# First phase of a hybrid layer: accumulators spilled through ScalarE and GpSimd, and the shift of the modulation summed on VectorE from the fourth block on

## The chip, the cores and the metric

The kernel runs on one core of a Trainium2 chip. The metric is the device time of one execution in microseconds. PE is TensorE, DVE VectorE, ACT ScalarE, POOL GpSimd, SP the queue that issues most of the loads.

## What is computed

One layer of a diffusion backbone on 256 latent tokens and 256 context tokens of 4096 channels, all float32. Cut to what matters here:

```python
mod_l = silu(c) @ w_ada + b_ada            # shift, scale and gate, 3 x 4096, for the latent tokens
mod_c = silu(c_ctx) @ w_ada + b_ada        # the same for the context tokens
hl = rmsnorm(xl, norm_g) * (1.0 + sc_l) + sh_l
hc = rmsnorm(xc, norm_g) * (1.0 + sc_c) + sh_c
# hl @ w_in and hc @ w_in: nine groups of columns; then convolution, recurrence and attention on them,
# the output projection, the gate g_l and a last rmsnorm
```

Shift and scale of a channel are needed before that channel's row of `w_in` can be used in a product, and they cost two columns of `w_ada` each, 134 MB in all.

## The kernel before, in words

**Phases.** The first phase (to about 941 us of the profile) computes r_x and v of both kinds of tokens and k of the context. The second phase computes the other columns of `w_in` with the convolution, the recurrence and the attention beside them, the third the output projection. Only the first phase is touched by the change, but for one buffer size.

**Blocks.** In the first phase the contraction over 4096 channels, 32 tiles of 128, is cut into ten blocks (`BLOCKS`: 1, 2, 3, 3, 3 and five of 4 tiles, counted from 0 here). In each block ten chunks of 512 columns are multiplied: two of kind "r" and four of "k" by `gemm_cm` (line 342), four of "v" by `gemm_tm` (line 361). A chunk leaves its result in four PSUM banks (r, v) or two (k), 32 in each block. `bank` gives the products five PSUM banks in turn. `spill` (line 492) moves a chunk's banks into accumulators `acc` in SBUF: in block 0 by a ScalarE copy (line 497), in all others by a VectorE addition that reads the bank and the accumulator (line 499).

**Weights.** `weights` loads `w_in` through SP into buffers `raw` (`NRAW` of them, shared with the loads of `w_ada`), and splits each pair of tiles into a high part on ScalarE (`hi`, line 338) and a low part on VectorE (`lo`, line 339). Each product runs as three passes over these parts. There are three buffers of `hi` and three of `lo`.

**Modulation.** `ada_units` (line 165) makes units of one load of up to 1 MB of `w_ada` each. A unit's work is either products on TensorE (line 217, tile `psa`, the two vectors as stationary columns) or, with `on_vector`, eight VectorE instructions that add a scaled row to one of two accumulators `gacc` (lines 160 and 162, one of each pair for the latent and one for the context vector). The finish `fin_` sends the sums through transposes on TensorE (line 175, tile `psm`; one set for `psa`, two sets for `gacc`) and reduces them on VectorE (lines 177 and 179). Part 0 of a block is the scale (`modG`), part 1 the shift (`modS`). Units of the next blocks are emitted between the products of this one by `background`, at a rate of 2.15 times the chunk's weight less 1.2. When both parts of a block are there, `make_h` (line 314) computes the normalised, modulated tokens of it (tiles `h`, `ch`, `lh`, lines 320 to 322).

**Order.** Every engine runs its instructions in the order that a scheduler wrote at build time; work within `hp()` is put as early as it can be. Pages of 2 KB a partition (`page`, `NPG` of them) hold the accumulators, tokens and all else that lives for a while.

**Last block.** In it `aside` puts the recurrence of the first heads among the chunks; its gate weights `gw` are loaded from GpSimd's queue (lines 425 and 426), and the sums for the gate g_l begin on VectorE (line 245).

Of the kernel before, what the change touches and what calls it, by code (L numbers as in the profile page):

```python
# [17 lines left out]
P = 128  # L18
# [6 lines left out]
    0, 1024, 2048, 3072, 4096, 5120, 7168, 9216, 11264)  # L25
# blocks of the contraction in the first phase, in tiles of 128
BLOCKS = [1, 2, 3, 3, 3, 4, 4, 4, 4, 4]
# from this block on, every second one's shift is summed on the vector engine
PAIRED = 8
# pages of 2 KB, buffers of weights as loaded and as split  # L30
NPG, NRAW, NHI = 75, 3, 3
# tiles of the contraction kept for the second half of the last chunk
HELD = 12
# urgency of what the tensor engine waits for
HP = 200000
# rates of the loads that go beside the products, by phase
ADA_A, ADA_B, CAP = 2.15, 1.2, 4.0
G1, G2, G3 = 0.4, 0.3, 0.4
# chunks of the last block that a recurrence follows; order of the second phase
REC1 = (1, 2, 4, 6, 8)  # L40
# [4 lines left out]
def tile_hybrid_layer(ctx: ExitStack, tc: tile.TileContext, x, c, cctx_tok, c_ctx, w_ada, b_ada,  # L45
                      norm_g, w_in, conv_w, conv_b, ln_g, ln_b, w_pw, b_pw, rconv_w, rconv_b,
                      w_r, b_r, w_i, b_i, lam, rpb, w_out, final_g, masks, out):
    nc = tc.nc
# [10 lines left out]
    def background(weight):  # L59
        """emits queued units of loads between those of the products, at the set rate"""  # L60
        bg["credit"] = min(bg["credit"] + bg["rate"](weight), CAP)
        while bg["q"] and bg["credit"] >= 2.0:
            bg["credit"] -= 2.0
            bg["q"].pop(0)()
# [17 lines left out]
    V, A, S, G = nc.vector, nc.scalar, nc.sync, nc.gpsimd  # L82
# [39 lines left out]

    # silu(c), silu(c_ctx) as channel columns, padded to 32 stationary columns
    scol = cp.tile([P, 64], F32, name="scol")
# [30 lines left out]
    def accumulate(k, w, n, which):  # L155
        """gacc[b] += silu(vector b)[k] * w on the vector engine"""
        for b in which:
            a, s = gacc[b][:, :n], scol[:, 32 * b + k:32 * b + k + 1]
            if k == 0:
                V.tensor_scalar(a, w, s, None, ALU.mult)  # L160
            else:
                V.scalar_tensor_tensor(a, w, s, a, ALU.mult, ALU.add)

# [1 line left out]
    def ada_units(k0, s, parts=(0, 1), on_vector=False):  # L165
# [92 lines left out]
    def rsqrt(y, v, t):  # L258
        """y = v ** -0.5, the table's root refined by a Newton step"""
        A.activation(y, v, AF.Sqrt)  # L260
        V.reciprocal(y, y)
        V.tensor_mul(t, y, y)
        V.tensor_mul(t, t, v)
        V.tensor_scalar(t, t, -0.5, 1.5, ALU.mult, ALU.add)
        V.tensor_mul(y, y, t)

# [1 line left out]
    ss = cp.tile([P, 4, 8], F32, name="ss")  # L268
# [56 lines left out]

# [1 line left out]
    def weights(view, ks, c0):  # L327
        """tiles of the weights, up to 4 loaded and 2 split at a time: [(tiles of the contraction, high, low)]"""
        for i in range(0, len(ks), 4):
            kp = ks[i:i + 4]  # L330
            raw = wp.tile([P, 4, 512], F32, name="raw", tag="raw", bufs=NRAW)
            S.dma_start(raw[:, :len(kp)], view[:, kp[0]:kp[0] + len(kp), c0:c0 + 512])
            for o in range(0, len(kp), 2):
                n = min(2, len(kp) - o)
                hi = wp.tile([P, 2, 512], F32R, name="hi", tag="hi", bufs=NHI)
                lo = wp.tile([P, 2, 512], F32R, name="lo", tag="lo", bufs=NHI)
                with hp():
                    A.copy(hi[:, :n], raw[:, o:o + n])  # L338
                    V.tensor_sub(lo[:, :n], raw[:, o:o + n], hi[:, :n].bitcast(F32))  # L339
                yield kp[o:o + n], hi, lo  # L340

    def gemm_cm(view, ks, c0, movs):
        """channel-major: out[n, t] for 4 tiles of n and each moving operand, 256 columns a region"""
        nb = 2 * len(movs)
        banks = [bank("g", "gcm") for _ in range(nb)]
        for kp, wh, wl in weights(view, ks, c0):
            for nt in range(4):
                for j, k in enumerate(kp):
                    last = k == ks[-1]
                    seq = [(wh, m, 0) for m in range(len(movs))] + [(wh, m, 1) for m in range(len(movs))] + \  # L350
                          [(wl, m, 0) for m in range(len(movs))]
                    for qi, (w, m, part) in enumerate(seq):
                        r = nt * len(movs) + m
                        first = k == ks[0] and qi < len(movs) and r % 2 == 0
                        nc.tensor.matmul(banks[r // 2][:, (r % 2) * T:(r % 2) * T + T],  # L355
                                         w[:, j, nt * P:(nt + 1) * P], movs[m][k][:, part],
                                         start=first, stop=last and qi >= 2 * len(movs), skip_group_check=True)
            background(len(movs))
        return banks

    def gemm_tm(view, ks, c0, stats, end=True):
        """token-major: out[t, n] for each stationary operand, 512 columns"""
        banks = [bank("g", "gtm") for _ in stats]
# [20 lines left out]
    def columns():  # L384
# [4 lines left out]
        V.tensor_scalar(hpw, col("b_pw", 0, 8), 0.5, None, ALU.mult)  # L389
        # 4 softplus(-lam), softplus(-lam) = (max(-lam, 0) + log1p(exp(-|lam|))), log1p(e) = 2 atanh(e / (2 + e))  # L390
        lm = col("lam", 0, 16)
# [21 lines left out]
    def ybs(n):  # L413
        """where the two directions' sum of head n lies: half a page of the inputs of a pair of heads"""
        return acc[("r", n // 4), n % 4 // 2 * 2][:, (n % 2) * T:(n % 2) * T + T]

    def recurrence(n):
# [22 lines left out]
        for d in range(2):  # L440
# [6 lines left out]
            A.activation(ti, pi, AF.Tanh, bias=hbi[:, ci:ci + 1], scale=0.5)  # L447
            # 2 sigmoid(z) = exp(min(z, 0)) (1 + |tanh(z / 2)|)
            A.activation(e, pr, AF.Relu, bias=nbr[:, ci:ci + 1], scale=-1.0)
# [31 lines left out]

# [1 line left out]
    acc = {}  # L483
    side = [lambda n=n: recurrence(n) for n in range(8)]

    def aside(n=1):
        """emits the next pieces of work that need few products, among the chunks of those that need many"""
        for _ in range(n):
            if side:
                side.pop(0)()  # L490

    def spill(banks, key):
        for i, b in enumerate(banks):
            with hp():
                if (key, i) not in acc:
                    acc[key, i] = page([P, 512], name="acc")
                    A.copy(acc[key, i], b)
                else:
                    V.tensor_add(acc[key, i], acc[key, i], b)  # L499

# [4 lines left out]
    while bi < len(BLOCKS):  # L505
        if bi < PAIRED:
            aq += ada_units(starts[bi], BLOCKS[bi])
        else:
            # the second block's shift is summed on the vector engine, spread among the other three parts
            pe = ada_units(starts[bi], BLOCKS[bi]) + [lambda bi=bi: done.add(bi)]  # L510
            bi += 1
            pe += ada_units(starts[bi], BLOCKS[bi], parts=(0,))
            ve = ada_units(starts[bi], BLOCKS[bi], parts=(1,), on_vector=True)
            for i, u in enumerate(pe):
                aq.append(u)
                n = len(ve) * (i + 1) // len(pe) - len(ve) * i // len(pe)
                aq += ve[len(ve) * i // len(pe):][:n]
        aq.append(lambda bi=bi: done.add(bi))
        bi += 1
# [37 lines left out]

# [1 line left out]
    ALLK = list(range(KT))  # L559
# [7 lines left out]
    def silu2(b):  # L567
        """2 silu(b), a page"""
        t = page([P, 512], name="sil")
# [50 lines left out]

    # queries lie from right to left within a grid row, so that the bias rows are read with a stride of +1
    def att_group(g):
# [120 lines left out]

# [1 line left out]
    korder = list(range(16, 32)) + list(range(8, 16)) + list(range(8))  # L745
# [3 lines left out]
    for oc in range(8):  # L749
# [27 lines left out]
        if oc < 7:  # L777
# [4 lines left out]
            continue  # L782
        # last chunk: the second token tile comes behind the first by HELD tiles of the contraction
        gate()
# [37 lines left out]
def _window():  # L822
    """neighbourhood mask by shape alone: rows are (query row parity, query column from the right),
    columns are key columns; a factor and an addend"""
    qc = 63 - np.arange(P) % 64
# [27 lines left out]
```

## Time and profile before

| | us |
|---|---|
| median of 3 runs | 2377.08 |
| lowest and highest | 2374.56, 2380.82 |
| span of the profiled execution, first to last instruction | 2371.5 |
| what lies around the span, median less span | 5.6 |
| TensorE busy | 2315.1 |
| VectorE busy | 1580.3 |
| ScalarE busy | 945.7 |
| GpSimd busy | 95.8 |

The page gives no other time for the profiled execution than its span; the table sets it beside the median. TensorE's ends of instructions are modelled, so that its work is read from the distance of starts and not from its busy share.

### The profile page before, as it was taken

The numbers are of one execution on the slowest core, as the hardware profiler recorded it, in microseconds if no ns is written. First come the engines' busy times: TensorE is split into PE (matmuls) and PEld (weight loads), VectorE is DVE, ScalarE is ACT, GpSimd is POOL, SyncE is SP. The second block draws the span as 40 slices with busy tenths as digits, with TensorE's granted clock in tenths as the row PEclk, the third lists the DMA queues.
The fourth block names the chain that finished last, engine by engine and source line by source line (L and its number), as shares of the span: only waits on it lengthen the run. The fifth ranks groups of instructions, "written<-read, shape, count | busy, mean of one in ns | idle before, by whom it ended". The sixth has DMA issues, their size and how long they took to land.

```text
span 2371.5 us, 38433 instructions
## 1 busy us (share of the span) xinstructions
PE 2315.1 (98%) x16013; PEld 2034.4 (86%) x16013; DVE 1580.3 (67%) x2289; ACT 945.7 (40%) x1228; POOL 95.8 (4%) x150
## 2 busy tenths in 40 slices
PE   6899999999999999999999999999999999999997
PEld 4667777777788998999999899999999999888886
DVE  4465545445778779987879596955766666665555
ACT  5322212222223246886433343344444434434444
POOL 0000000000000001000000101101001001000000
PEclk9999999999999999999999999999999999999999
DMA  9888788877877544656776767767576678775664
GB/s 312 270 279 272 254 298 298 295 266 252 295 269 258 192 163 174 222 183 213 245 233 203 188 215 202 204 215 188 182 245 171 207 265 301 264 263 187 191 192 173
DMA packets 293461, 551.27 MB, mean 232 GB/s; under 512 B 10959, under 2 KB 52647, under 8 KB 293287
## 3 DMA queue, kind: packets, MB, share of 16 engines
q1 hardware_dynamic: 287856, 536.91, 66.1%
q0 software_dynamic: 4480, 11.54, 4.3%
q8 instruction: 125, 2.05, 0.3%
q10 hardware_dynamic: 951, 0.37, 0.1%
q14 instruction: 49, 0.40, 0.0%
HBM read 544.58 MB, written 4.19 MB: 231 GB/s over the span
## 4 chain that ended last, share of the span: by engine, by line
PE 83%; DMA 8%; DVE 4%; ACT 3%; issue 1%; SPq 0%; DVEq 0%; ACTq 0%
PE gcm L355 48%; PE gtm L371 9%; PE gtm L372 8%; PE gtm L370 8%; PE psa L217 5%; DMA raw<-in_w_ada_dram 4%; DMA raw<-in_w_in_dram 3%; DVE lo L339 2%; PE y L614 1%; ACT hi L338 1%; DMA xp<-in_ctx_dram 1%; DVE gacc L245 1%; PE pt L607 1%; PE sc L593 0%; PE sc L594 0%
## 5 line engine op out<-in xcount | busy, mean ns | idle before, releaser
L339 DVE TENSOR_TENSOR lo<-raw,hi 128x1024 fp32r<-128x1024 f32 (+1 forms) x630 | 747.4, 1189 | 556.8 <-ACT hi L338 552.9
L338 ACT CAST hi<-raw 128x1024 fp32r<-128x1024 f32 (+1 forms) x630 | 640.1, 1022 | 1171.9 <-PE gcm L355 492.8
L355 PE MATMUL gcm<-lh,hi 128*128 128x256 f32 x5632 | 1069.5, 285 | 2.9 <-ACT hi L338 2.8
L355 PEld LDWEIGHTS gcm<-lh,hi 128*128 128x128 f32 x5632 | 896.8, 192 | 18.3 <-issue 13.4
L355 PE MATMUL gcm<-lh,lo 128*128 128x256 f32 x2816 | 796.2, 285 | 4.2 <-DVE lo L339 4.0
L355 PEld LDWEIGHTS gcm<-lh,lo 128*128 128x128 f32 x2816 | 537.8, 192 | 11.6 <-DVE lo L339 5.8
L355 PE MATMUL gcm<-ch,hi 128*128 128x256 f32 x1536 | 326.6, 287 | 3.4 <-ACT hi L338 2.3
L355 PEld LDWEIGHTS gcm<-ch,hi 128*128 128x128 f32 x1536 | 259.0, 191 | 36.3 <-issue 27.8
L245 DVE SCALAR_TENSOR_TENSOR gacc<-raw,scol,gacc 128x512 f32<-128x512 f32 x248 | 185.8, 749 | 49.6 <-DMA raw<-in_w_ada_dram 47.1
L355 PE MATMUL gcm<-ch,lo 128*128 128x256 f32 x768 | 217.6, 286 | 0.0
L371 PE MATMUL gtm<-lo,mix 128*128 128x512 f32 x488 | 192.0, 393 | 0.1
L372 PE MATMUL gtm<-hi,mix 128*128 128x512 f32 x488 | 190.1, 390 | 0.0
L370 PE MATMUL gtm<-hi,mix 128*128 128x512 f32 x488 | 171.1, 390 | 0.0
L355 PEld LDWEIGHTS gcm<-ch,lo 128*128 128x128 f32 x768 | 146.5, 191 | 12.8 <-issue 9.0
L217 PE MATMUL psa<-raw,cpad 128*32 128x512 f32 (+3 forms) x1216 | 132.5, 521 | 7.9 <-DMA raw<-in_w_ada_dram 7.8
L499 DVE TENSOR_TENSOR acc<-acc,gcm 128x512 f32<-128x512 f32 x144 | 96.1, 682 | 37.7 <-PE gcm L355 37.1
L371 PEld LDWEIGHTS gtm<-lo,mix 128*128 128x128 f32 x488 | 91.6, 188 | 20.5 <-DVE lo L339 1.3
L370 PEld LDWEIGHTS gtm<-hi,mix 128*128 128x128 f32 x488 | 91.5, 188 | 19.2
L499 DVE TENSOR_TENSOR acc<-acc,gtm 128x512 f32<-128x512 f32 x144 | 94.3, 680 | 19.9 <-PE gtm L372 19.7
L372 PEld LDWEIGHTS gtm<-hi,mix 128*128 128x128 f32 x488 | 91.7, 188 | 18.4
L673 DVE SCALAR_TENSOR_TENSOR cv<-upad,cols,cv 128x256 f32<-128x256 f32 x240 | 105.6, 483 | 0.0
L371 PE MATMUL gtm<-lo,ch 128*128 128x512 f32 x256 | 102.2, 399 | 0.2 <-DVE lo L339 0.2
(218 smaller groups left out, 2107.9 us busy)
## 6 DMA issues: line engine op xcount, KB each, us to landing
raw<-in_w_in_dram SPq DMA_DIRECT2D x210, 1024.0 KB, 5.2
raw<-in_w_ada_dram SPq DMA_DIRECT2D x156, 1024.0 KB, 5.5
raw<-in_w_out_dram SPq DMA_DIRECT2D x61, 1024.0 KB, 5.5
raw<-in_w_ada_dram SPq DMA_DIRECT2D x48, 768.0 KB, 5.9
raw<-in_w_in_dram SPq DMA_DIRECT2D x30, 768.0 KB, 6.1
raw<-in_w_in_dram SPq DMA_DIRECT2D x10, 512.0 KB, 5.4
xp<-in_ctx_dram SPq DMA_DIRECT2D x16, 256.0 KB, 5.8
xp<-in_x_dram SPq DMA_DIRECT2D x16, 256.0 KB, 5.4
```

What stands on the lines that cost most here:

```text
L217: nc.tensor.matmul(st["ps"][32 * q:32 * q + 32, :W], cpad[k // 16][:, k % 16, :], raw[:, j, :], start=(k < 4), stop=(k >= KT - 4))
L245: V.scalar_tensor_tensor(st["a"], raw[:, j], s, st["a"], ALU.mult, ALU.add)
L338: A.copy(hi[:, :n], raw[:, o:o + n])
L339: V.tensor_sub(lo[:, :n], raw[:, o:o + n], hi[:, :n].bitcast(F32))
L355: nc.tensor.matmul(banks[r // 2][:, (r % 2) * T:(r % 2) * T + T], w[:, j, nt * P:(nt + 1) * P], movs[m][k][:, part], start=first, stop=las ...
L370: nc.tensor.matmul(banks[b], hh, wh[:, j], start=first, stop=False)
L371: nc.tensor.matmul(banks[b], hh, wl[:, j], start=False, stop=False)
L372: nc.tensor.matmul(banks[b], hl, wh[:, j], start=False, stop=last)
L499: V.tensor_add(acc[key, i], acc[key, i], b)
L607: nc.tensor.transpose(ps[:, kt * T + qt * P:kt * T + qt * P + P], Ps[qt][:, (2 * kp + kt) * P:(2 * kp + kt + 1) * P], ident)
L614: nc.tensor.matmul(ps[:, :T], acc[("v", h // 4), kt][:, i * P:(i + 1) * P], Ps[kt // 2][:, (kt % 2) * T:(kt % 2) * T + T], start=(kt == 0) ...
L673: V.scalar_tensor_tensor(o, upad[n][:, tap:tap + T], cw(tap, n), o, ALU.mult, ALU.add)
```

## The change

Three things are done to the first phase, and two sizes make room for them.

- `spill` no longer adds on VectorE. From block 1 on each bank is copied to a page `sum` by ScalarE (line 500 of the changed kernel), and GpSimd adds that page to the accumulator (line 501).
- The shift of every block from 3 on is summed on VectorE. Before, that was so for block 9 alone, and the shifts of blocks 3 to 8 went to TensorE.
- Units of the scale (TensorE) and of the shift (VectorE) of one block now alternate.
- Buffers `raw` go from 3 to 4 and pages from 75 to 77; the memory comes from the scratch of the DMAs that GpSimd issues, set to 4096 bytes.

```diff
-PAIRED = 8
+ON_VECTOR = 3
-NPG, NRAW, NHI = 75, 3, 3
+NPG, NRAW, NHI = 77, 4, 3
...
                     A.copy(acc[key, i], b)
                 else:
-                    V.tensor_add(acc[key, i], acc[key, i], b)
+                    t = page([P, 512], name="sum")
+                    A.copy(t, b)
+                    G.tensor_add(acc[key, i], acc[key, i], t)
...
-        if bi < PAIRED:
+        if bi < ON_VECTOR:
             aq += ada_units(starts[bi], BLOCKS[bi])
         else:
-            pe = ada_units(starts[bi], BLOCKS[bi]) + [lambda bi=bi: done.add(bi)]
-            bi += 1
-            pe += ada_units(starts[bi], BLOCKS[bi], parts=(0,))
+            pe = ada_units(starts[bi], BLOCKS[bi], parts=(0,))
             ve = ada_units(starts[bi], BLOCKS[bi], parts=(1,), on_vector=True)
-            for i, u in enumerate(pe):
-                aq.append(u)
-                n = len(ve) * (i + 1) // len(pe) - len(ve) * i // len(pe)
-                aq += ve[len(ve) * i // len(pe):][:n]
+            for i in range(len(ve)):
+                aq += pe[len(pe) * i // len(ve):len(pe) * (i + 1) // len(ve)]
+                aq.append(ve[i])
         aq.append(lambda bi=bi: done.add(bi))
         bi += 1
...
-    nc = _bacc.Bacc("TRN2", target_bir_lowering=False, num_devices=1)
+    nc = _bacc.Bacc("TRN2", target_bir_lowering=False, num_devices=1, dynamic_dma_scratch_size=4096)
```

VectorE in the middle of the first phase, blocks of four tiles. Before, the low parts (`lo`) stand between additions of PSUM banks to accumulators:

```order
L499 TENSOR_TENSOR acc_588<-acc_588,gcm_3859 128x512
L339 TENSOR_TENSOR lo<-raw,hi 128x1024 x2
L499 TENSOR_TENSOR acc_620<-acc_620,gcm_3988 128x512
L499 TENSOR_TENSOR acc_622<-acc_622,gcm_3989 128x512
L339 TENSOR_TENSOR lo<-raw,hi 128x1024
L170 COPY adas_120<-psa_3845 128x512
L339 TENSOR_TENSOR lo<-raw,hi 128x1024
L499 TENSOR_TENSOR acc_656<-acc_656,gtm_4056 128x512
```

Of the change, the low parts stand between the sums of the shift:

```order
L339 TENSOR_TENSOR lo<-raw,hi 128x1024
L162 SCALAR_TENSOR_TENSOR gacc_126<-raw,scol,gacc_126 128x512
L339 TENSOR_TENSOR lo<-raw,hi 128x1024
L162 SCALAR_TENSOR_TENSOR gacc_125<-raw,scol,gacc_125 128x512
L162 SCALAR_TENSOR_TENSOR gacc_126<-raw,scol,gacc_126 128x512
L179 TENSOR_REDUCE sums_4532<-psm_4533 128x8
L339 TENSOR_TENSOR lo<-raw,hi 128x1024
L183 TENSOR_TENSOR modG<-sums_4532,cols 128x8
```

The additions of banks have left VectorE's queue, and instructions that read two operands from SBUF (`raw` and `gacc`) stand in their place.

ScalarE at the same place. Before, its queue holds the high parts and little else:

```order
L338 CAST hi<-raw 128x1024
L321 ACTIVATE ch_4657<-h_4656,modS 128x256
L338 CAST hi<-raw 128x1024 x11
L321 ACTIVATE lh_4658<-h_4656,modS 128x256
L321 ACTIVATE ch_4666<-h_4665,modS 128x256
```

Of the change, the copies of a chunk's banks (`gcm` two, `gtm` four) stand between the high parts:

```order
L338 CAST hi<-raw 128x1024
L500 COPY sum_5555<-gtm_5472 128x512
L500 COPY sum_5558<-gtm_5473 128x512
L500 COPY sum_5561<-gtm_5474 128x512
L500 COPY sum_5564<-gtm_5475 128x512
L338 CAST hi<-raw 128x1024 x2
L500 COPY sum_5637<-gcm_5567 128x512
L338 CAST hi<-raw 128x1024
L500 COPY sum_5640<-gcm_5568 128x512
```

A high part now waits behind copies, and these wait for the chunk's last product and for a free page.

GpSimd at the end of the first phase. Before, the loads of the recurrence's gate weights are its first work after the memsets at the start:

```order
L133 MEMSET cpad_100 128x512
L152 MEMSET adas_119 128x512
L152 MEMSET adas_120 128x512
L152 MEMSET junk_121 128x512
L425 DMA gw_7680<-in_w_r_dram 128x128
L426 DMA gw_7680<-in_w_i_dram 128x128
```

Of the change, these loads stand among the additions of the last block:

```order
L425 DMA gw_8422<-in_w_r_dram 128x128
L426 DMA gw_8422<-in_w_i_dram 128x128
L501 TENSOR_TENSOR acc_620<-acc_620,sum_8534 128x512
L501 TENSOR_TENSOR acc_622<-acc_622,sum_8537 128x512
L425 DMA gw_8423<-in_w_r_dram 128x128
L426 DMA gw_8423<-in_w_i_dram 128x128
```

There are 288 such additions on GpSimd, and in the last block some of them stand behind a load that waits until an earlier head's gate weights have been used.

## Rows read from the trace of the kernel before

**Rows 1.** Busy time and share of the span by engine, whole execution.

```profile
PE 2315.1 (98%) x16013; PEld 2034.4 (86%) x16013; DVE 1580.3 (67%) x2289; ACT 945.7 (40%) x1228; POOL 95.8 (4%) x150
```

**Rows 2.** Busy time in four stretches, all engines: block 1, blocks 2-7, 8, 9.

```profile
core 0: us, PE busy (x) PEld busy (x) DVE busy (x) ACT busy (x) POOL busy (x), PEclk, DMA share, GB/s
95.00:165.40 70.40, 67.33 (x461) 48.49 (x460) 43.40 (x96) 14.18 (x18) 0.00 (x0) 0.98 0.82 271
165.40:756.70 591.30, 590.57 (x3871) 450.95 (x3870) 349.54 (x535) 135.83 (x173) 1.57 (x3) 1.00 0.81 278
756.70:849.00 92.30, 92.30 (x601) 84.73 (x600) 64.86 (x84) 22.06 (x21) 0.70 (x2) 1.00 0.56 196
849.00:941.50 92.50, 92.50 (x550) 79.87 (x549) 81.20 (x116) 52.30 (x66) 7.52 (x14) 1.00 0.47 163
```

**Rows 3.** The same view of line 499 alone (VectorE), blocks 2-7.

```profile
165.40:756.70 591.30, 126.66 (x193) 1.00 0.81 278
```

**Rows 4.** TensorE in order of time (start, duration, line, tiles), around modulation products.

```profile
126.31 0.39 PE L371 MATMUL gtm<-lo,lh 128*128 128x512 f32 x1
126.63 0.85 PE L217 MATMUL psa<-raw,cpad 128*32 128x384 f32 x8
127.41 0.50 PE L372 MATMUL gtm<-hi,lh 128*128 128x512 f32 x1
127.75 0.39 PE L370 MATMUL gtm<-hi,lh 128*128 128x512 f32 x1
...
399.86 0.28 PE L355 MATMUL gcm<-lh,hi 128*128 128x256 f32 x1
399.98 0.28 PE L355 MATMUL gcm<-ch,hi 128*128 128x256 f32 x1
400.19 1.06 PE L217 MATMUL psa<-raw,cpad 128*32 128x512 f32 x8
401.19 0.38 PE L355 MATMUL gcm<-lh,hi 128*128 128x256 f32 x1
401.41 0.28 PE L355 MATMUL gcm<-ch,lo 128*128 128x256 f32 x1
```

**Rows 5.** VectorE in order of time: seven sums of the shift.

```profile
603.58 4.73 DVE L162 SCALAR_TENSOR_TENSOR gacc<-raw,scol,gacc 128x512 f32<-128x512 f32 x7 [3.87 <-DMA raw<-in_w_ada_dram]
```

**Rows 6.** VectorE's groups, blocks 2-7: busy, mean ns | idle before, releasers.

```profile
L339 DVE TENSOR_TENSOR lo<-raw,hi 128x1024 fp32r<-128x1024 f32 x92 | 112.4, 1223 | 177.3 <-ACT hi L338 177.3
L162 DVE SCALAR_TENSOR_TENSOR gacc<-raw,scol,gacc 128x512 f32<-128x512 f32 x62 | 43.1, 744 | 6.7 <-DMA raw<-in_w_ada_dram 6.6
L339 DVE TENSOR_TENSOR lo<-raw,hi 128x512 fp32r<-128x512 f32 x29 | 19.9, 687 | 5.0 <-ACT hi L338 4.9
```

**Rows 7.** One line's instructions: duration ns min/median/max, first and last start.

```profile
L497 ACT COPY acc<-gcm x16: 579/590/616, 52.1 to 80.9; 128x512 f32<-128x512 f32 x16
...
L588 POOL TENSOR_TENSOR B<-B,mask x16: 992/1010/1982, 1223.8 to 1803.6; 128x384 f32<-128x384 f32 x16
```

**Rows 8.** GpSimd's groups, whole execution: busy, mean ns | idle before.

```profile
L133 POOL MEMSET cpad<- 128x512 f32 x2 | 1.0, 519 | 0.0
...
L679 POOL MEMSET om<- 128x128 f32 x1 | 0.2, 205 | 0.0
```

**Rows 9.** GpSimd and VectorE in order of time where both run, second phase.

```profile
1524.53 2.85 POOL L587 TENSOR_TENSOR B<-B,mask 128x384 f32<-128x384 f32 x1 [6.55 <-DMA B<-in_rpb_dram]
1527.46 1.08 POOL L588 TENSOR_TENSOR B<-B,mask 128x384 f32<-128x384 f32 x1
...
1525.29 1.22 DVE L339 TENSOR_TENSOR lo<-raw,hi 128x1024 fp32r<-128x1024 f32 x1
1526.42 2.40 DVE L673 SCALAR_TENSOR_TENSOR cv<-upad,cols,cv 128x256 f32<-128x256 f32 x2
...
1466.01 0.88 DVE L673 SCALAR_TENSOR_TENSOR cv<-upad,cols,cv 128x256 f32<-128x256 f32 x2
...
1802.38 1.18 POOL L587 TENSOR_TENSOR B<-B,mask 128x384 f32<-128x384 f32 x1 [5.41 <-DMA B<-in_rpb_dram]
...
1802.59 1.52 DVE L245 SCALAR_TENSOR_TENSOR gacc<-raw,scol,gacc 128x512 f32<-128x512 f32 x1
```

## The prediction

> **What bounds the kernel now.** I read the shares first: TensorE is busy 98% of the span, VectorE 67%, ScalarE 40%, GpSimd 4% [rows 1]. Since TensorE's ends are modelled, I then looked at its starts in the first phase: 256-column products start every 0.12 us (399.86, 399.98) and 512-column ones every 0.23, without gaps [rows 4]. In blocks 2 to 7, 591.3 us, TensorE is busy 590.6 at a granted clock of 1.00, VectorE 349.5 (59%), ScalarE 135.8, GpSimd idle but for 1.6, the DMA engines at 0.81 [rows 2]. So TensorE sets the pace there; whatever leaves it is gained for as long as all others keep up, and VectorE has 242 us to spare. Block 9 is different: VectorE is at 81.2 of 92.5 us there, because of the recurrence [rows 2].
>
> **The change, part by part.** All sums are made for the profiled span, 2371.5 us; 5.6 us lie between it and the median of the runs.
>
> *Products taken off TensorE.* A unit of four tiles shows as a run of eight records (two for each float32 product). With 512 columns it delays its neighbours from 399.98 to 401.41, 1.43 us where two steps of 0.12 would do: 1.19 us. For 384 columns it is 126.31 to 127.75 less two steps of 0.23: 0.98 us [rows 4]. A part of a block (scale or shift) runs over 32 tiles, so eight such units. Six shifts leave: blocks 5 to 8 with 512 columns, 3 and 4 with 384, so 32 x 1.19 + 16 x 0.98 = 53.8 us. A shift summed on VectorE needs two sets of transposes instead of one, 22 more at some 0.11 us (128 columns at the rate of the rest, an estimate): 2.4. TensorE gains 51 us and needs 540 for these six blocks.
>
> *Sums added to VectorE.* Seven sums of 512 columns take 4.73 us, the last of them 0.74, so they start 0.665 apart [rows 5, 6]. By the two sizes of the low part, 1223 and 687 ns for 1024 and 512, an element costs 1.05 ns [rows 6], so 384 columns start 0.53 apart (estimate). By the changed order the six stretches hold 310 sums of 512 and 114 of 384, where the kernel before has 62 of 512: 248 x 0.665 + 114 x 0.53 = 225 us more. Six copies of `psa` go, 4 us less.
>
> *Additions taken off VectorE.* 126.7 us in the six blocks [rows 3]. VectorE then has 349.5 - 126.7 + 225 - 4 = 444 us of work, 82% of 540.
>
> *Copies on ScalarE.* 32 a block at 0.59 us [rows 7], 113 us, so ScalarE is busy 249 of 540: covered, priced at nothing. But it is a queue: a copy waits for the chunk's last product and for a free `sum` page, and behind it stand the next high parts, for these the low parts on VectorE, and then TensorE. The built program lets a copy run five or six additions ahead of GpSimd in blocks 2 to 8, and one or two ahead in most of block 9.
>
> *Additions on GpSimd.* No such addition of 512 columns is in the trace. The nearest rows are the mask's, 384 columns, two SBUF operands: 0.99 us at the least, median 1.01 [rows 7]. GpSimd's memsets, 519 ns for 512 and 205 for 128 columns, give a fixed 0.10 us [rows 8]; so 0.10 + 0.91 x 512/384 = 1.31 us each (estimate), 252 us for the 192 of the six blocks. GpSimd alone has the room. The question is what they do to VectorE.
>
> *The two engines side by side.* At 1526.42 two VectorE sums, which take 0.88 when nothing else runs, take 2.40 while two GpSimd operations pass; GpSimd's first one, 2.85 instead of 1.0, had waited until the low part ended at 1526.51. At 1802.59 a sum into `gacc`, the very instruction that the change multiplies, takes 1.52 instead of 0.74: it ends 0.55 after GpSimd's does [rows 9]. So they take turns. Low parts, sums, tokens `h`: nearly all that is left on VectorE reads two SBUF operands, while the additions taken off read one from PSUM. A GpSimd operation of 384 costs a full VectorE queue (2.40 - 0.88)/2 = 0.76 us; in proportion 1.01 for 512, the lower price. The whole 1.31 is the upper one; a price of nothing is the first rival's.
>
> The Trainium skill says as much ("SBUF — State Buffer", "SBUF: two separate sides"): GpSimd and VectorE share a pair of ports, held by one of them for a whole instruction, also against a VectorE instruction with two SBUF inputs. By that rule alone, each addition shutting VectorE out for its whole length, the sum would be the upper price's; without the rule it would be the first rival's. The page says that whoever starts first gets the pair; in the row GpSimd waited 1.9 us through several VectorE instructions, so the trace agrees with the exclusion and shows that the turns are not even.
>
> *The sum of blocks 2 to 7.* VectorE and GpSimd together: 444 + 192 x 1.01 = 638 us, or 444 + 252 = 696, against 540 of TensorE. TensorE would wait for low parts. The change is then 638 - 591 = +47 to +105 us. I take 655, +64: nearer to the lower price, because VectorE's queue is as full here as in its row, plus 17 us since no queue is full all the time (it waits for `hi` and for loads).
>
> *Other blocks.* Block 1: 43 us of VectorE less 21 of additions, plus 32 x 1.01 and ten sums of 0.53, some 60 of 70 us: nothing. Block 8: 65 - 21 + 32 = 76 of 92: nothing. Block 9: 81 - 21 + 32 = 92 of 92.5, just full, with few pages and with gate loads in GpSimd's queue that wait for earlier heads: 0 to 20, I take 4.
>
> *The fourth raw buffer.* In block 1 TensorE idles 3 us [rows 2]; a load more in flight may give back 0 to 8 us over the kernel, I take 3. The smaller scratch concerns GpSimd's loads only, most of them issued long ahead of need: nothing, 5 us at worst.
>
> Sum: +64 + 4 - 3 = +65, a span of 2436 and a time of **2442 us**.
>
> **The rivals.**
>
> *The additions fit in the gaps (faster).* If the two engines hardly met, TensorE would stay the bound: -51 - 3 = -54, a time of 2323. For it: VectorE's 82% leaves 96 us, and its queue pauses, as the 177 us of idling before low parts show [rows 6]. Against it: 638 us of work that exclude each other do not go into 540. It decides if an addition costs VectorE under (540 - 444)/192 = 0.50 us, half the lower price.
>
> *A draw.* At 0.77 us an addition the six blocks come out at 591 again and the whole within 0.3%, about what a measurement of this kernel can tell from no change (7 us): 2370 to 2384.
>
> *ScalarE held up by pages (slower still).* If each addition waits as at 1524.53, 1.85 us before 1.31 of work, GpSimd needs 32 x 3.16 = 101 us a block. The three blocks of three tiles want 80 or so, copies run out of pages, high parts stall behind them, and VectorE idles while it should work: the 696 us at 95% use are 733, +142, with 10 more in block 9: 2371.5 + 152 + 5.6 = 2529.
>
> *The change doesn't do what it says.* The order shows 288 additions on GpSimd and the sums on VectorE, so I give this nothing.
>
> **How the numbers follow.** Forecast (+20 to +120, 2397 to 2497) 0.58; fits in the gaps 0.22, at 2323 to 2370; draw 0.08; pages 0.12. Predicted 2442. The range must leave out no more than 2 in 10: it starts at 2345, half way between the first rival and no change, and ends at 2500, the upper price of the sum with little more. Faster by over 0.3%: 0.23; within: 0.09; slower: 0.68.
>
> **What would show it.** Right: in blocks 2 to 7 TensorE shows idle time released by `lo` (line 339); means of the sums and low parts rise well over 744 and 1223 ns; the `sum` additions on GpSimd show medians over 1.3 us; first spill of block 2 to that of block 8 takes some 655 us. Wrong: TensorE dense there and the stretch near 540 us, with sums at 744 ns; that would mean that the two engines don't shut each other out as in the second phase. If the stretch is longer and ScalarE waits for GpSimd most, it is the pages.

## The result and the profile after

The changed kernel takes 2473.6 us (median of 4 runs, 2470.7 to 2476.1) against 2376.4 before (median of 4): a ratio of 1.040, 95% interval 1.039 to 1.042. The profiled execution spans 2471.0 us against 2371.5. The forecast was 2442 and slower.

Where the time went, by the start of each block's first spill (an addition on VectorE before, a copy to a `sum` page after), block 9 to the end of the last one:

| us | before | after | difference | predicted |
|---|---|---|---|---|
| block 1 | 70.4 | 71.1 | +0.7 | 0 |
| blocks 2 to 7 | 591.3 | 669.6 | +78 | +64 (47 to 105) |
| block 8 | 92.3 | 98.0 | +6 | 0 |
| block 9 | 92.7 | 114.2 | +22 | +4 (0 to 20) |
| all behind the first phase | 1429.9 | 1423.5 | -6 | -3 (0 to -8), whole kernel |

The first line of the page, and then the same stretch as in [rows 2], blocks 2 to 7, all engines of the changed kernel:

```profile
PE 2312.4 (94%) x15651; PEld 2056.7 (83%) x15651; DVE 1849.7 (75%) x2385; ACT 1101.1 (45%) x1516; POOL 555.1 (22%) x438
```

```profile
core 0: us, PE busy (x) PEld busy (x) DVE busy (x) ACT busy (x) POOL busy (x), PEclk, DMA share, GB/s
166.30:836.00 669.70, 583.42 (x3533) 471.46 (x3532) 609.73 (x719) 236.94 (x356) 311.31 (x192) 0.95 0.71 245
```

TensorE was dense there before (590.6 of 591.3); now it idles 86 us, and VectorE is busy 609.7 of 669.7 us. The granted clock fell from 1.00 to 0.95, that is, TensorE ran at the lower of its two levels (1.2 GHz instead of 2.4) for about a tenth of the stretch, with pauses that it did not have before. What TensorE waited for in the same stretch (waiter, releaser: us in total, times, longest):

```profile
PE psa L217 <- DMA raw<-in_w_ada_dram: 28.2, 16, 4.0
PE gcm L355 <- DVE lo L339: 23.6, 11, 5.3
PE gcm L355 <- ACT hi L338: 10.0, 4, 4.1
PE psm L175 <- DVE adas L170: 9.3, 5, 4.1
PE gtm L371 <- DVE lo L339: 7.0, 5, 4.2
```

Over half of the 86 us is VectorE's at once, the low parts above all. The 28 us for loads of `w_ada` can be VectorE's too, by way of the `raw` buffers (experiments 6 and 7). Groups of VectorE in the stretch (busy, mean ns, idle before), to set beside [rows 6]:

```profile
L162 DVE SCALAR_TENSOR_TENSOR gacc<-raw,scol,gacc 128x512 f32<-128x512 f32 x310 | 288.2, 983 | 40.0 <-DMA raw<-in_w_ada_dram 40.0
L339 DVE TENSOR_TENSOR lo<-raw,hi 128x1024 fp32r<-128x1024 f32 x91 | 125.6, 1381 | 2.4 <-ACT hi L338 2.4
L162 DVE SCALAR_TENSOR_TENSOR gacc<-raw,scol,gacc 128x384 f32<-128x384 f32 x112 | 90.3, 857 | 9.4 <-DMA raw<-in_w_ada_dram 9.4
L339 DVE TENSOR_TENSOR lo<-raw,hi 128x512 fp32r<-128x512 f32 x29 | 30.5, 1050 | 0.0
L160 DVE TENSOR_SCALAR gacc<-raw,scol 128x512 f32<-128x512 f32 x10 | 10.1, 1047 | 7.6 <-DMA raw<-in_w_ada_dram 7.6
```

A sum that took 744 ns takes 983 on average, a low part 1381 instead of 1223, one of 512 columns 1050 instead of 687. And before, VectorE idled 177 us for `hi` ahead of the low parts; now 2.4: it no longer waits for ScalarE, only for loads, 57 us ahead of the sums and of the scalings that start them (line 160). Here is what lengthens the instructions, VectorE and GpSimd in order of time in block 5:

```profile
569.11 8.85 DVE L162 SCALAR_TENSOR_TENSOR gacc<-raw,scol,gacc 128x512 f32<-128x512 f32 x7
...
568.92 1.41 POOL L501 TENSOR_TENSOR acc<-acc,sum 128x512 f32<-128x512 f32 x1 [5.87 <-ACT sum L500]
571.55 5.19 POOL L501 TENSOR_TENSOR acc<-acc,sum 128x512 f32<-128x512 f32 x3 [1.23 <-ACT sum L500]
```

Seven sums alone took 4.73 us [rows 5]. With four additions among them they take 8.85: 4.12 us for four, 1.03 each. That is the lower price of the prediction, 1.01, at the place itself. GpSimd waits as well. All its additions (min/median/max ns):

```profile
L501 POOL TENSOR_TENSOR acc<-acc,sum x288: 1261/1584/3158, 95.2 to 1049.9; 128x512 f32<-128x512 f32 x144
```

The shortest is 1.26 us where 1.31 was estimated.

Which VectorE instructions are held up can be read in block 9, where two of one kind stand side by side: line 456 reads both operands from SBUF, line 457 reads one of them from PSUM (`pr`).

```profile
1001.24 1.76 DVE L456 SCALAR_TENSOR_TENSOR rec<-rec,rec 128x512 f32<-128x512 f32 x1
1002.93 0.68 DVE L457 SCALAR_TENSOR_TENSOR rec<-pr,rec 128x512 f32<-128x512 f32 x1
...
1000.21 2.24 POOL L501 TENSOR_TENSOR acc<-acc,sum 128x512 f32<-128x512 f32 x1
1002.97 1.30 POOL L501 TENSOR_TENSOR acc<-acc,sum 128x512 f32<-128x512 f32 x1
```

Both run beside an addition; the first takes 1.76 us instead of 0.69, the second its usual 0.68.

TensorE's waits in block 9, and ScalarE's for GpSimd there, are of another kind than in blocks 2 to 7:

```profile
PE gtm L370 <- ACT sum L500: 4.5, 3, 2.2
PE pr L444 <- DVE rec L438: 3.5, 2, 2.0
PE gcm L355 <- ACT sum L500: 2.3, 1, 2.3
```

```profile
ACT sum L500 <- POOL acc L501: 6.1, 5, 1.8
```

No low part and no load is among them. TensorE waited 6.8 us until copies had emptied a PSUM bank, and 3.5 us for the recurrence; some of the copies had waited for GpSimd to free a page.

### The profile page after: what moved, and what is told of

The parts are those of the page before. It is cut to its first block, busy times and chain, and to the rows that moved or that the text cites. A ratio compares the mean times of both kernels' runs of the same rounds, so it can differ in the third digit from the quotient of the medians.

```text
span 2471.0 us, 38734 instructions
## 1 busy us (share of the span) xinstructions
PE 2312.4 (94%) x15651; PEld 2056.7 (83%) x15651; DVE 1849.7 (75%) x2385; ACT 1101.1 (45%) x1516; POOL 555.1 (22%) x438
## 4 chain that ended last, share of the span: by engine, by line
PE 57%; DVE 24%; DMA 12%; issue 4%; ACT 2%; SPq 0%; DVEq 0%; ACTq 0%
PE gcm L355 38%; DVE gacc L162 11%; DMA raw<-in_w_ada_dram 10%; DVE lo L339 6%; PE gtm L371 5%; PE gtm L372 5%; PE gtm L370 5%; DVE gacc L245 1%; DMA raw<-in_w_in_dram 1%; PE y L612 1%; DMA xp<-in_ctx_dram 1%; DVE h L320 1%; PE psa L217 1%; ACT hi L338 1%; DVE ch L322 1%
## 5 line engine op out<-in xcount | busy, mean ns | idle before, releaser
L339 DVE TENSOR_TENSOR lo<-raw,hi 128x1024 fp32r<-128x1024 f32 (+1 forms) x630 | 789.3, 1256 | 368.9 <-ACT hi L338 358.0
L501 POOL TENSOR_TENSOR acc<-acc,sum 128x512 f32<-128x512 f32 x288 | 460.8, 1620 | 565.2 <-ACT sum L500 563.9
L162 DVE SCALAR_TENSOR_TENSOR gacc<-raw,scol,gacc 128x512 f32<-128x512 f32 (+1 forms) x434 | 387.2, 945 | 49.4 <-DMA raw<-in_w_ada_dram 49.4
L355 PE MATMUL gcm<-ch,hi 128*128 128x256 f32 x1536 | 342.2, 296 | 19.8 <-ACT hi L338 10.0
L355 PEld LDWEIGHTS gcm<-ch,hi 128*128 128x128 f32 x1536 | 271.9, 202 | 50.9 <-issue 18.5
L245 DVE SCALAR_TENSOR_TENSOR gacc<-raw,scol,gacc 128x512 f32<-128x512 f32 x248 | 198.5, 801 | 89.4 <-DMA raw<-in_w_ada_dram 86.9
L500 ACT COPY sum<-gcm 128x512 f32<-128x512 f32 x144 | 83.5, 587 | 118.5 <-PE gcm L355 110.9
L582 POOL DMA_DIRECT2D B<-in_rpb_dram x32 | 21.2, 666 | 502.9 <-DVE sc L594 377.5
L217 PE MATMUL psa<-raw,cpad 128*32 128x512 f32 (+3 forms) x832 | 92.0, 536 | 28.6 <-DMA raw<-in_w_ada_dram 28.4
L500 ACT COPY sum<-gtm 128x512 f32<-128x512 f32 x144 | 81.0, 588 | 66.6 <-PE gtm L372 58.5
```

The source lines that it names most:

```text
L217: nc.tensor.matmul(st["ps"][32 * q:32 * q + 32, :W], cpad[k // 16][:, k % 16, :], raw[:, j, :], start=(k < 4), stop=(k >= KT - 4))
L245: V.scalar_tensor_tensor(st["a"], raw[:, j], s, st["a"], ALU.mult, ALU.add)
L500: A.copy(t, b)
L501: G.tensor_add(acc[key, i], acc[key, i], t)
```

## The experiments

The theory under test: VectorE and GpSimd take turns whenever both read SBUF, so that their work adds up, and the sum passes TensorE's. Rivals: the copies on ScalarE and the few pages; the sums of the shift crowding VectorE by themselves; the buffer sizes. Times are medians, in brackets the ratio to the kernel before, measured again beside each run (2373.9 to 2376.4 us), with its 95% interval. Blocks are measured as in the table above.

**1. The sizes alone.** The kernel before with

```diff
-NPG, NRAW, NHI = 75, 3, 3
+NPG, NRAW, NHI = 77, 4, 3
...
-    nc = _bacc.Bacc("TRN2", target_bir_lowering=False, num_devices=1)
+    nc = _bacc.Bacc("TRN2", target_bir_lowering=False, num_devices=1, dynamic_dma_scratch_size=4096)
```

> The kernel before with only the sizes of the change: four raw buffers, 77 pages, the smaller scratch. The stretch after the first phase was 9.4 us shorter in the changed kernel. Theory (the fourth raw buffer gives that back): 6 to 12 us under the kernel before, about 2367. Rival (it came from the new order, not from the buffers): within 3 us of the kernel before.

2364.1 us (0.996, 0.995 to 0.997). The new sizes are a gain of their own, about 9 us by the ratio, most of it behind the first phase (1421.4 against 1429.9 in the profiled runs). Which of the three sizes gives it was not separated. The part of the change that looked like a side matter is the only one that pays alone, and the other experiments are to be set beside 2364.

**2. The spill alone.** Experiment 1 with

```diff
-                    V.tensor_add(acc[key, i], acc[key, i], b)
+                    t = page([P, 512], name="sum")
+                    A.copy(t, b)
+                    G.tensor_add(acc[key, i], acc[key, i], t)
```

> The sizes of the change and the spill through ScalarE and GpSimd; the modulation as in the kernel before. Theory (VectorE and GpSimd take turns and only their sum counts): in blocks 2 to 7 VectorE has 349.5 - 126.7 = 223 us and the 192 additions cost 1.0 to 1.3 us each, 417 to 475 together against 591 of TensorE, so these blocks stay at 591 within 5; only block 9, full in the kernel before, grows by 10 to 25. Whole: 2376 to 2392 with the gain of the buffers. Rival (the copies on ScalarE and the few pages hold up the high parts): blocks 2 to 7 grow by 30 us or more, whole over 2410.

2408.7 us (1.015, 1.013 to 1.016), 45 over experiment 1, and blocks 2 to 7 take 616 us, 24 more than with the sizes alone. That is neither forecast: more than a plain sum of 417 to 475 us under 591 allows, less than the rival's 30 in blocks 2 to 7. 17 of the 24 us fall in blocks 6 and 7 (226 against 209), where the shift of block 9 is summed on VectorE in this kernel too, the other 7 in block 2, and block 9 itself takes 114.3 against 96.2. So in blocks 2 to 7 most of the cost lies where VectorE has more two-operand work than the low parts. Yet over blocks 6 and 7 VectorE is not full, 147 of 226 us, its waits for GpSimd included, and GpSimd 98 (all engines):

```profile
550.20:776.50 226.30, 215.62 (x1358) 173.73 (x1357) 147.40 (x159) 83.88 (x121) 98.29 (x64) 0.97 0.68 242
```

TensorE idles 10.7 us there, 6.3 of them for loads of `w_ada`, 2.7 for `adas` (the copy of `psa`) and 1.6 for a low part; the clock, 0.97 instead of 1.00, makes up the other 7 of the 17 us (an estimate: 0.03 x 226). With the sizes alone TensorE had no such wait in these blocks. Why the loads are late with VectorE at 65% is not settled. Waiting for pages isn't it: ScalarE waited for GpSimd 8.6 us in all, 1.6 in these two blocks and 5.9 in block 9.

```profile
  ACT sum L500: 517.1, 150
  PE gcm L355: 76.0, 74
  PE gtm L372: 63.0, 67
  POOL acc L501: 8.6, 8
```

(Idle time of the engines ahead of instructions on the tile `sum`, by releaser, whole execution: the first line is GpSimd waiting for copies, the last ScalarE waiting for a free page.)

**3. The shift alone.** The change with the spill put back:

```diff
-                    t = page([P, 512], name="sum")
-                    A.copy(t, b)
-                    G.tensor_add(acc[key, i], acc[key, i], t)
+                    V.tensor_add(acc[key, i], acc[key, i], b)
```

> The change with the spill put back to additions on VectorE; the shift on VectorE from block 3 on stays. Theory (the port): GpSimd has no work in the first phase, so sums and low parts run at their own length (741 and 1223 ns); VectorE has 444 + 127 = 571 us for blocks 2 to 7 against 540 of TensorE, so the blocks take 571 to 600 and the whole is 2345 to 2380, some 100 us under the changed kernel. Rival (the sums alone crowd VectorE's queue): blocks 2 to 7 stay over 640, whole over 2440.

2376.2 us (1.001, 1.000 to 1.002), 97 under the change and 12 over experiment 1. GpSimd has no part in it, so the shift on VectorE is no gain even so: blocks 2 to 7 take 604 us, 4 over the range that was given. The worst is block 4, 110.5 us against 91.9 with the sizes alone (all engines, and what TensorE waited for most):

```profile
336.90:447.40 110.50, 90.05 (x532) 70.03 (x531) 99.51 (x157) 19.65 (x28) 0.00 (x0) 0.91 0.73 257
```

```profile
PE gcm L355 <- ACT hi L338: 13.3, 3, 5.4
PE gcm L355 <- DVE h L320: 4.7, 1, 4.7
```

VectorE is busy 99.5 of 110.5 us and TensorE no longer dense. It waits for high parts, and ScalarE waited 58 us for the loads of these. Alone, the shift costs 12 us and the spill 45 over the sizes; together they cost 110. The two parts get in each other's way.

**4. No additions.** The change without GpSimd's additions, the copies left in:

```diff
-                    G.tensor_add(acc[key, i], acc[key, i], t)
```

> The change without GpSimd's additions: the copies to the sum pages stay, the accumulators keep block 0 only. Theory (the port, or anything else that GpSimd's additions bring): VectorE's 444 us fit into TensorE's 540, blocks 2 to 7 fall from 670 to 540 to 560, sums return to 741 ns, the whole is 2310 to 2345. Rival (copies on ScalarE or sums on VectorE by themselves): blocks 2 to 7 stay over 630, whole over 2430.

2333.6 us (0.984, 0.981 to 0.986), 140 under the change. Blocks 2 to 7, all engines, and VectorE's sums and low parts:

```profile
158.20:712.50 554.30, 545.54 (x3533) 450.30 (x3532) 452.83 (x719) 237.63 (x357) 0.00 (x0) 0.99 0.85 297
```

```profile
L162 DVE SCALAR_TENSOR_TENSOR gacc<-raw,scol,gacc 128x512 f32<-128x512 f32 x310 | 213.6, 745 | 36.1 <-DMA raw<-in_w_ada_dram 36.1
L339 DVE TENSOR_TENSOR lo<-raw,hi 128x1024 fp32r<-128x1024 f32 x92 | 112.2, 1220 | 40.0 <-ACT hi L338 33.4 <-PE gcm L355 6.3
```

The same 719 instructions on VectorE now take 453 us instead of 610, and each is back at its old length. The copies on ScalarE (238 us busy, as in the change) cost next to nothing in these blocks: TensorE waited 2.9 us for `hi`.

**5. Memsets for additions.** GpSimd is kept busy and the page held as long, but nothing is read from SBUF:

```diff
-                    G.tensor_add(acc[key, i], acc[key, i], t)
+                    for _ in range(3):
+                        G.memset(t, 0.0)
```

> The change with each GpSimd addition replaced by three memsets of the sum page, 1.56 us of GpSimd by the memset's row (0.52 each), so that a page is held longer than by an addition of 1.3; the accumulators keep block 0 only. These memsets write SBUF and read nothing. Theory (what shuts VectorE out is GpSimd's reading of SBUF): blocks 2 to 7 at 554 to 570 as without additions, sums at 741 ns, whole 2330 to 2350. Rival (pages held by GpSimd, or GpSimd's work of any kind): blocks 2 to 7 over 640, whole over 2440.

2341.8 us (0.987, 0.985 to 0.989), 8 over experiment 4 and 132 under the change.

```profile
160.90:713.10 552.20, 544.86 (x3532) 450.66 (x3531) 454.31 (x719) 237.61 (x357) 285.86 (x577) 0.99 0.86 299
```

```profile
L162 DVE SCALAR_TENSOR_TENSOR gacc<-raw,scol,gacc 128x512 f32<-128x512 f32 x310 | 213.5, 743 | 33.8 <-DMA raw<-in_w_ada_dram 33.7
```

```profile
L502 POOL MEMSET sum<- 128x512 f32 x864 | 431.5, 528 | 454.9 <-ACT sum L500 420.3 <-DVE sums L177 11.2 <-DVE ch L322 5.7
```

GpSimd is busy 286 us in the stretch, nearly the 311 of the change, and VectorE's sums don't feel it: 743 ns, and the memsets take 528 where the kernel before shows 519. So what shuts VectorE out of two-operand work is not GpSimd's work of any kind, and not the time a page is held; it is, of the two operations tried, the one that reads SBUF. The Trainium skill ("SBUF — State Buffer", "SBUF: two separate sides") says so of VectorE instructions with two SBUF inputs, that they collide only with a GpSimd operation that reads SBUF; these rows agree. The 14 scalings of line 160, which read one tensor from SBUF, are an exception: with memsets the longest takes 761 ns, without additions 488.

**6. More pages, and three raw buffers.** The change with

```diff
-NPG, NRAW, NHI = 77, 4, 3
+NPG, NRAW, NHI = 81, 3, 3
```

> The change with three raw buffers and 81 pages instead of four and 77: four more sum pages, the same memory. Theory (the port): pages don't matter; the fourth raw buffer was worth 9 us, so 2474 to 2490. Rival (copies that wait for pages): under 2450, and ScalarE no longer waits for GpSimd.

2547.0 us (1.072, 1.071 to 1.074): no gain by pages, but a loss of 73 us. Both forecasts missed.

**7. Three raw buffers, pages as in the change.**

```diff
-NPG, NRAW, NHI = 77, 4, 3
+NPG, NRAW, NHI = 77, 3, 3
```

> The change with three raw buffers instead of four and the 77 pages it has. With 81 pages and three raw buffers it took 2547. If pages don't matter and only the raw buffer does: 2530 to 2565. If the four more pages gave something back: over 2570. If it was the pages that did harm, by the order that they bring: under 2510.

2551.1 us (1.074, 1.072 to 1.076). So the four more pages were worth about 4 us, little more than the noise of the two medians. By the profiles nothing of it lies in blocks 2 to 7 (729 us with more pages, 728 without), and all of it in block 9 (115.2 against 119.4), where ScalarE waited for GpSimd 7.7 us with 77 pages and not at all with 81. So the rival of the pages falls for blocks 2 to 7 and keeps a few us in block 9; 81 pages with four raw buffers were not run. The fourth raw buffer is worth 77 us in the change; in the kernel before, it and the other two sizes together gave 9. SP's queue in blocks 2 to 7 shows whom the loads wait for:

```profile
SPq L332 <- DVE gacc L162: 119.9, 22, 13.0
SPq L195 <- DVE gacc L162: 102.3, 15, 11.4
SPq L195 <- DVE lo L339: 94.1, 25, 12.0
```

A raw buffer is given back by VectorE, after the sums or low parts that read it. By these waits, when VectorE is late, loads are late, then high parts (`hi`: ScalarE waited 192 us for loads of `w_in`), then TensorE (67 us of waits for `hi`).

**8. Half additions.** The change with additions of 256 columns:

```diff
-                    G.tensor_add(acc[key, i], acc[key, i], t)
+                    G.tensor_add(acc[key, i][:, 0:256], acc[key, i][:, 0:256], t[:, 0:256])
```

> The change with each GpSimd addition cut to 256 of the 512 columns (the other half of the accumulators keeps block 0). By the memset's fixed part and the mask's slope such an addition takes 0.71 us instead of 1.31. Theory (VectorE loses the time for which an addition runs): of the 140 us that the additions cost in all (2474 against 2334 without them) a share of 0.71/1.31 or less stays, 2395 to 2412. Rival (a price for each instruction, whatever its length: hand-over, the copy, the page): over 2450.

2381.0 us (1.002, 1.001 to 1.003), 14 below the range. The shortest such addition takes 0.72 us, as estimated:

```profile
L501 POOL TENSOR_TENSOR acc<-acc,sum x288: 720/958/2743, 95.9 to 954.1; 128x256 f32<-128x256 f32 x144
```

A price for each instruction, whatever its length, is ruled out. But the cost is not in proportion either: with 0.72/1.26 = 57% of the length, 47 of 140 us are left, 34%. VectorE itself lost 69 us in blocks 2 to 7 (522.2 busy against 452.8), 44% of the 157 that it loses in the change, and TensorE's loss is less again. That fits a threshold, VectorE having some time free and only what goes beyond it delaying TensorE, but nothing here shows that it is one. TensorE's waits for loads of `w_ada` in blocks 2 to 7 lie between as well: 19.7 us here, 4.8 in experiment 4, 28.2 in the change.

**9. The last block's spill on VectorE.** The change with

```diff
...
+                    if key[2]:
+                        V.tensor_add(acc[key[:2], i], acc[key[:2], i], b)
+                        continue
                     t = page([P, 512], name="sum")
...
-            spill(bk, (kind, i))
+            spill(bk, (kind, i, not more))
```

(Elsewhere in `spill`, `key` becomes `key[:2]`.)

> The change with the last block's spill put back to additions on VectorE, the others as in the change. In block 9 the changed kernel took 114.2 us, without additions 103.1, with VectorE's additions 96.2. Theory (copies, additions and gate loads crowd a block in which VectorE is full): block 9 takes 95 to 99 and the whole falls by 14 to 20, to 2454 to 2460; the other blocks stay. Rival (block 9 is long because of what the blocks ahead leave undone): block 9 stays over 108 and the whole over 2466.

2454.7 us (1.033, 1.032 to 1.035), 19 under the change, block 9 back to 95.4 us, each of the others within 1.5 of the change. Without additions it was 103.1 (experiment 4), with memsets 108.8, with additions 114.2. So some 8 of the 19 us come with the new spill without additions, by its copies or its order; some 6 come with memsets too, which read nothing but hold the pages; and only some 5 need an operation that reads SBUF. In the change GpSimd idled 12 us in block 9 ahead of gate loads (`gw`) and ScalarE 6.1 us for pages; how much of that reached TensorE was not separated.

**10 and 11. Less of the shift on VectorE.** Both keep the new sizes and the spill on VectorE; the shift goes to VectorE for the blocks named (`(6, 9)` in the second):

```diff
-ON_VECTOR = 3
+ON_VECTOR = (3, 6, 9)
...
-        if bi < ON_VECTOR:
+        if bi not in ON_VECTOR:
```

> A version that might beat both: the sizes of the change, the spill on VectorE, and the shift on VectorE for blocks 3, 6 and 9 only, alternating with the scale. With the shift of all blocks from 3 on (and the spill on VectorE) the blocks in which those of 3 and 6 are loaded were 4 and 8 us shorter than with the buffers alone, and the others not. Theory (VectorE must keep some tenth of its time free): 2350 to 2360, 5 to 14 us under the buffers alone (2364). Rival (whatever goes to VectorE costs as much as TensorE gains): 2364 or more.

2364.8 us (0.995, 0.994 to 0.997): over the forecast of 2350 to 2360, and no better than the sizes alone.

> The same with the shift on VectorE for blocks 6 and 9 only. Theory: 2353 to 2362. Rival: 2364 or more.

2358.7 us (0.994, 0.991 to 0.996), as forecast, and the lowest of all that compute the whole. It beats both kernels; against experiment 1 (0.995 to 0.997) the intervals overlap, so that the shift of one more block on VectorE is worth a few us at most, and nothing certain. Blocks 2 to 7 take 589 us against 592; with block 3 added, 596.

## Why the prediction was right, and what it mis-sized

**The bound.** Right. TensorE, dense before, now waits for VectorE, at once and, it seems, through loads that VectorE holds up.

**Products off TensorE: 51 us.** The direction is right, and it could not be had in full. Without additions blocks 2 to 7 take 554 us, 38 under experiment 1. TensorE's own busy time there is 545.5 (540 predicted); the rest is pauses of TensorE, with VectorE at 82%.

**VectorE's own work: 444 us.** Measured without contention: 452.8.

**ScalarE's copies at nothing.** Right in blocks 2 to 7 (experiment 4), wrong in block 9: TensorE waited 6.8 us there for banks that copies had still to empty.

**An addition: 1.31 us, 1.01 of it VectorE's loss in a full queue.** 1.26 and 1.03. On average over the stretch the loss is (609.7 - 452.8)/192 = 0.82, probably because some additions ran while VectorE had nothing to read.

**The sum, +64.** +78, inside 47 to 105, but partly by luck, since two errors offset each other. The predicted 655 us are 444 + 194 of additions + 17 of idle time; the measured 670 are 453 + 157 + 60. The lower price, applied to all 192 additions, was 37 us too much. The 17 us for a queue that is not full all the time were 43 too little: VectorE idled 57 us ahead of sums and scalings whose loads had not come. The rows of the kernel before could have told: 6.7 us for 62 sums [rows 6], in proportion 46 for 422 (an estimate). These waits hardly grew by the additions; experiment 4 has 52 us of them, where VectorE has time to spare. They stayed when VectorE had become the engine that the others wait for, and there they cost. Whether late buffers make them is not shown.

**Block 9, +4.** The term that was wrong by most: +22, beyond its bound of 20. The sum counted VectorE's time, 92 of 92.5 us, as what decides. But VectorE was busy 96.4 of 114.2 us, and TensorE waited for no low part: it idled 12 us, 6.8 of them for PSUM banks that copies on ScalarE had not emptied and 3.5 for the recurrence, and ran at a clock of 0.96. ScalarE's queue, in which the copies stand among the recurrence, was not in the sum, and the few pages and gate loads that the prediction did name were put too low. Experiment 9 agrees: only some 5 of its 19 us need additions that read SBUF. The rest of the 22 us stays open. Block 8 was predicted at 0 and took 6 us more; TensorE waited there only for low parts, 5.6 us.

**The fourth raw buffer, -3.** All three sizes together gave -9, just over the bound of 8; in the change the buffer alone stands for 77 us.

**The rivals.** "The additions fit in the gaps" fell: an addition costs VectorE 0.82 on average and 1.03 at a full queue, over the 0.50 from which it would have been right. "A draw" asked for 0.77, on the prediction's sum; the measured 0.82 lies just over it. By the price alone, then, the six blocks would have come out some 19 us longer (453 + 157 = 610 against 591); the other 60 of the 78 us are VectorE's idle time. "ScalarE held up by pages" fell for blocks 2 to 7, where ScalarE waited for GpSimd 0.8 us. In block 9 it was 6.1 of the 10.2 us of the whole execution, and the 4 us that four more pages moved lie there.

**The clock.** Not predicted and not separated. The 0.95 in blocks 2 to 7 is at most 0.05 x 670 = 33 us of work at the full level; it goes with TensorE's pauses, and with additions gone it is 0.99.

## What to carry to other kernels

Before work is moved from VectorE to GpSimd, look at what the rest of VectorE's instructions read: if they take two operands from SBUF, and the GpSimd operation reads SBUF, the two engines take turns, and the work moved costs VectorE up to most of its length on the slower engine (1.03 of 1.26 us here, 0.82 on average). An instruction that reads one operand from PSUM was not held up (line 457), so such an addition is a good one to keep on VectorE. And a queue that hands back load buffers needs slack: TensorE waited little with VectorE 82% busy (experiment 4) and much at 90% (block 4 of experiment 3), though in experiment 2 it was late already at 65%, so that the mean share alone doesn't decide. What was late seems to come back as late loads: with three load buffers instead of four the change lost another 77 us.

## What the runs showed of the hardware

GpSimd's memsets (0.53 us, nothing read) ran beside VectorE's two-operand sums with hardly a cost to either, 743 and 528 ns, while additions of the same page cost VectorE 1.03 us each in a full queue. VectorE instructions that read one operand from PSUM passed beside additions too: line 457 took 677 to 692 ns in all its 16 runs in the change, line 456, with two from SBUF, up to 1761. But reading a single tensor from SBUF is not enough to be free of it: the 512-column scalings of line 160 took 482 ns without additions (experiment 4) and 1047 on average with them.
